# One more slot for weight slabs, taken from two chunk tiles, and a later rounding of the first unit's second slab

## The chip, the cores and the metric

The kernel runs on one core of a Trainium2 chip. The metric is the device time of one execution, in microseconds (us). Five engines work side by side, each through its own instructions in order: TensorE (PE, matmuls; PEld is its weight loads), VectorE (DVE), ScalarE (ACT), GpSimd (POOL) and SyncE (SP). Engines wait for each other by semaphores. SP and POOL issue most of the DMA transfers here.

## What is computed

The reference is one decoder layer on a sequence of 512 rows of width 1024, in fp32:

```python
# h = x + 1/2 * SwiGLU_1(rmsnorm(x))                # D_FF = 2816
# u = rmsnorm(h);  z = u @ W_in -> conv GLU | q | k | v | merge gates
# branch A: GLU -> causal depthwise conv (31 taps) -> LayerNorm -> swish -> C->D
# branch B: dilated causal window attention, 12 heads in 3 groups -> D
# h = h + W_o( sigmoid(gA) * yA + sigmoid(gB) * yB )
# h = h + 1/2 * SwiGLU_2(rmsnorm(h))
# h = h + sigmoid(rmsnorm(h) @ W_pg) * (p @ W_pp)
# y = rmsnorm_final(h)
def swiglu(x, w_gate, w_up, w_down):
    return (jax.nn.silu(x @ w_gate) * (x @ w_up)) @ w_down
```

The change alters no arithmetic.

## The kernel before, in words

**Precision.** PE multiplies rounded fp32 ("fp32r"). Each operand is split in a rounded high part and a remainder, and each product is made of three: high by high, high by low, low by high. `wr` is a raw weight slab, `wh` and `wl` its high and low part; `xsh` and `xsl` are those of an activation chunk `u`. The simple way to split is ACT's copy to `wh` (L398, L419, L540) and DVE's subtraction to `wl` (L399, L420, L541).

**The FFNs.** Each runs after the same list, PLAN: rounds `gate_up(j)` ("gu", j = 2 to 10), rounds `down` ("dn") and two rounds `down_plain` ("dp"); the two gate_up rounds ahead of them are made chunk by chunk while the input arrives. The end of the list is `dn 4, dp 0, gu 10, dp 1, dn 5`. A gate_up round multiplies with a scheme of seven products in place of eight, in the order B11, B21, T2, T1, T3, B22, T4 (`quarters_of`, L745, L746 for the high parts of the weights and L748 for the low ones; results in the PSUM banks pa, pe and pd). Behind each product ACT copies the bank (L943), or DVE adds the bank to an earlier copy (L956); L961, L965 and L966 scale, apply silu and multiply; L948 takes T4. What comes out is cut again into the forms that `down` needs by L676, L688 and L691. `down` runs the same seven products (L755, L756, L760) and DVE adds to the residual (L769, L771). `down_plain` is plain (PE L1004, L1005, L1008; DVE L1013).

**Weights.** `load_one` sends the quarters of a weight to raw slabs from SP's queue (L267). `sum_one` makes the sums that the seven products need on DVE (L336, L340, L344, L349). Products T2, T1, T3, B22 are split by L398 and L399. For B11, B21, T4 and dp the low part is made by DMA: ACT writes the negated high part to `wl` (L368), POOL issues a transfer that adds the raw slab to it (L370, the accumulating DMA), and ACT writes `wh` (L382).

**Slots.** All of these slabs, and the products `u`, come from one ring in on-chip memory: tag "w", `NW` slots of 128 x 1024 fp32, 4 KB a partition. Activation chunks come from a second ring, tag "t", `NT` slots of 128 x 512, 2 KB a partition. A tile that is asked for takes the free slot that was released first, and its first writer waits for whoever used the slot last. So an instruction can wait for an engine or a DMA whose data it never touches.

**Order.** The order of the instructions of each engine is that of the program as it is written (the scheduler is manual). Work beside the products is put between them by budgets (`work`, `spend`) that do not depend on the number of slots.

**The start.** `begin` loads eight input chunks and the first unit's two slabs on SP's and ACT's queues, and for each chunk `scaled` makes `u` (ACT L497) and `xsh`, `xsl` (DVE L498, L499). The slabs are rounded in three parts between them (`part`, L540 on ACT, L541 on DVE): part 0 is chunks 0 and 1 of the first slab, part 1 chunks 2 and 3, part 2 the whole second slab, which serves chunks 4 to 7.

Of the kernel before, what the change touches and what calls it, by code (L numbers as in the profile page):

```python
# [39 lines left out]
MAGIC = float(0x5F3759DF)  # L40


NT = 61
SLAB = 1024
NW = 16
RAW = 4
AHEAD = 2

# [101 lines left out]
def block_kernel(ctx: ExitStack, tc: tile.TileContext, a, out):  # L150
# [12 lines left out]
    def name(n):  # L163
        count[0] += 1
        return f"{n}_{count[0]}"

    def T(n, dt=F32, w=S):
        return act.tile([P, w], dt, name=name(n), tag="t", bufs=NT)

    def by_class(t):

        return t.rearrange("p (i c) -> p c i", c=NB)
# [24 lines left out]
    def quarter(n, step, q):  # L199

        x_, y = divmod(q, 2)
        if step[0] == "gu":
            w = a["w_ffn%s_%s" % (n, ("gate", "up")[x_])]
            return row_of([w[c][:, y * S:(y + 1) * S] for c in chunks(step[1])])
        if step[0] == "mx":
            return rows("w_mix_out", x_, 4 * y + 2 * step[1])
        return rows("w_ffn%s_down" % n, x_, 2 * ROUNDS[step[1]][0] + 2 * y)
# [50 lines left out]
    def W(n, dt=F32):  # L258
        return wts.tile([P, SLAB], dt, name=name(n), tag="w", bufs=NW)

# [18 lines left out]
    def load_one(hold=False):  # L279
        i = state["load"]  # L280
        key = order[i]
        q = product(key)
        if key[0] == "gq" or q is None:
            raws[i] = fetch(sources(key), first_=key[0] in POOLED or key[0] == "gq" and by_dma(key), hold=hold)
        elif q == "B11":
            for z in (A21, A22, A11):
                quarters[key[:2], z] = fetch(quarter(key[0], key[1], z))
        elif q == (MIXED if key[0] == "m" else PRODUCTS)[1]:
            quarters[key[:2], A12] = fetch(quarter(key[0], key[1], A12))
        state["load"] = i + 1  # L290
# [97 lines left out]
    def split_one():  # L388
        i = state["split"]
        if i in halves:  # L390
            state["split"] = i + 1
            return
        r, q, kind = raws.pop(i), product(order[i]), order[i][0]
        if q is not None:
            w = r.shape[-1]
            h, l = W("wh", F32R)[:, :w], W("wl", F32R)[:, :w]
            spend(0.25 + w * 0.00075, 0.17 + w * 0.001)
            A.activation(h, r, AF.Copy)  # L398
            V.tensor_sub(l, r, h.bitcast(F32))  # L399
            halves[i] = h, l  # L400
        elif kind == "pg":
            hs, ls, low = [], [], W("wl", F32R)
            for c in range(2):
                z = r.rearrange("p (m k i) -> p k m i", k=2, i=P)[:, c]
                h, l = T("pgh", F32R), low[:, c * S:(c + 1) * S]
                hm, lm = (t.rearrange("p (m i) -> p m i", i=P) for t in (h, l))
                A.activation(hm, z, AF.Copy)
                V.tensor_sub(lm, z, hm.bitcast(F32))
                hs.append(h)
                ls.append(l)  # L410
            halves[i] = (hs, ls)
        else:
            w = r.shape[-1]
            h, l = W("wh", F32R)[:, :w], W("wl", F32R)[:, :w]
            halves[i] = (h, l)
            if kind == "pT":
                r = r.rearrange("p (k i c) -> p k c i", k=2, c=NB)
                h, l = (z.rearrange("p (k c i) -> p k c i", k=2, c=NB) for z in (h, l))
            A.activation(h, r, AF.Copy)  # L419
            V.tensor_sub(l, r, h.bitcast(F32))  # L420
        state["split"] = i + 1
# [72 lines left out]
    def scaled(src, n, scale, by=lambda t: t):  # L494

        u, h, l = T("u"), T(n + "h", F32R), T(n + "l", F32R)
        A.activation(by(u), src, AF.Copy, scale=scale)  # L497
        V.tensor_copy(h, u)  # L498
        V.tensor_sub(l, u, h.bitcast(F32))  # L499
        return u, (h, l)  # L500
# [19 lines left out]
    def gain(v, c):  # L520
        return gains[:, v + c:v + c + 1]

    def begin():

        rs_ = [W("wr") for _ in range(2)]
        hl = [(W("wh", F32R), W("wl", F32R)) for _ in rs_]
        x = [res[:, :S] if c == 0 else T("x") for c in range(KD)]
        xs, us = [], {}
        cuts = [[(0, slice(0, 256)), (0, slice(512, 768))], [(0, slice(256, 512)), (0, slice(768, 1024))],
                [(1, slice(0, 512)), (1, slice(512, 1024))]]  # L530

        def piece(j, queue):
            for i, c in cuts[j]:
                g, at = divmod(c.start, S)
                src = quarter("1", ("gu", 0), (A11, A12)[i])[g][2]
                queue.dma_start(rs_[i][:, c], src[:, at:at + c.stop - c.start])

        def part(j):
            for i, c in cuts[j]:
                A.activation(hl[i][0][:, c], rs_[i][:, c], AF.Copy)  # L540
                V.tensor_sub(hl[i][1][:, c], rs_[i][:, c], hl[i][0][:, c].bitcast(F32))  # L541

        nc.sync.dma_start(gx[:, :V_DW + S], a["gx"])
        piece(0, nc.scalar)
        for c in range(1, KD):
            nc.sync.dma_start(x[c], a["xT"][c - 1])
            if c in (1, 3):
                piece((c + 1) // 2, nc.sync)
        nc.sync.dma_start(ident, a["eye"])
        state["load"] = state["sum"] = state["early"] = state["split"] = 2  # L550
        load_one()
        load_one()
        nc.sync.dma_start(taps, a["taps"])
        nc.sync.dma_start(freq, a["cst"][:, C_M[NG]:C_M[NG] + 1])
        for c in range(KD):
            us[c], z = scaled(by_class(x[c]), "xs", gain(V_G1, c), classes)
            xs.append(z)
            if c < 3:
                part(c)
            if c == HOLD:  # L560
                load_one(True)
            if c == KD - 1:
                split_one()
        halves[0], halves[1] = hl
        return x, xs, us
# [487 lines left out]
    def tables():  # L1053
        ip = act.tile([P, S], I32, name="ipos", tag="t", bufs=NT)
        nc.sync.dma_start(ip, bass.AP(tensor=a["positions"].tensor, offset=a["positions"].offset, ap=[[0, P], [1, S]]))
        ang, n, nh, nl, e = T("ang"), T("n"), T("nh", F32R), T("nl"), T("e")
        sin, cos = e, nl
        tabs["sin"], tabs["cos"] = sin, cos
        c = TWO_PI

        def do(f, *p, **q):
            bg.append(lambda: f(*p, **q))

        def less(t, k, w):
            do(V.scalar_tensor_tensor, t, k, -w, t, op0=OP.mult, op1=OP.add)

        def reduce(t):
            do(V.tensor_scalar, n, t, 1.0 / (2.0 * math.pi), ROUND, op0=OP.mult, op1=OP.add)
            do(V.tensor_scalar, n, n, -ROUND, None, op0=OP.add)
            for w in c[:3]:  # L1070
                less(t, n, w)

        do(V.tensor_copy, classes(ang), by_class(ip))
        do(V.tensor_scalar, ang, ang, freq, None, op0=OP.mult)
        do(V.tensor_scalar, ip, ang, 1.0 / (2.0 * math.pi), None, op0=OP.mult)
        do(V.tensor_copy, n, ip)
        do(V.tensor_copy, nh, n)
        do(V.tensor_sub, nl, n, nh.bitcast(F32))
        hi = nh.bitcast(F32)
        for k, w in ((hi, c[0]), (nl, c[0]), (hi, c[1])):  # L1080
            less(ang, k, w)
        do(V.tensor_scalar, e, nl, -c[1], None, op0=OP.mult)
        less(e, hi, c[2])
        reduce(ang)
        reduce(e)
        do(V.tensor_add, ang, ang, e)
        for k, w in ((nl, c[2]), (hi, c[3]), (nl, c[3])):
            less(ang, k, w)
        reduce(ang)
        do(V.tensor_scalar, ang, ang, 3.1415925, -3.1415925, op0=OP.min, op1=OP.max)  # L1090

        def end():
            A.activation(sin, ang, AF.Sin)
            V.scalar_tensor_tensor(n, ang, -1.0, ang, op0=OP.mult, op1=OP.max)
            V.tensor_scalar(n, n, -1.0, math.pi / 2, op0=OP.mult, op1=OP.add)
            A.activation(cos, n, AF.Sin)
            V.tensor_scalar(sin[0:64], sin[0:64], -1.0, None, op0=OP.mult)
        bg.append(end)


    norm = Rows()
    x, xs, u1 = begin()

    def row_block(b, j):
# [475 lines left out]
    for j in range(4):  # L1580
        wh, wl = slab(("ao", j))
        for i in range(2):
            m = 2 * j + i
            p = bank("pb")
            for kk in range(4):
                c = slice((4 * i + kk) * P, (4 * i + kk + 1) * P)
# [220 lines left out]
```

## Time and profile before

| what | us |
|---|---|
| median of 3 runs | 1279.35 |
| lowest and highest | 1276.61, 1281.44 |
| profiled execution | 1279.57 |
| its span | 1277.8 |
| PE busy in it | 1261.8 |

The span runs from the first to the last instruction that the profile has; 1.8 us of the execution lie around it. All times in the trace count from the span's start. FFN1 takes about the first 350 us, the mixing stage runs to about 840, FFN2 to about 1200, and the embedding and the last norm to the end. In rows of the timeline the columns are start, length, engine, line, operation, output and inputs by tile names without numbers, how many were grouped, and in brackets the idle time before it and what ended it.

### The profile page before, as it was taken

The numbers are of one execution on the slowest core, as the hardware profiler recorded it, in microseconds if no ns is written. First come the engines' busy times: TensorE is split into PE (matmuls) and PEld (weight loads), VectorE is DVE, ScalarE is ACT, GpSimd is POOL, SyncE is SP. The second block draws the span as 40 slices with busy tenths as digits, with TensorE's granted clock in tenths as the row PEclk, the third lists the DMA queues.
The fourth block names the chain that finished last, engine by engine and source line by source line (L and its number), as shares of the span: only waits on it lengthen the run. The fifth ranks groups of instructions, "written<-read, shape, count | busy, mean of one in ns | idle before, by whom it ended". The sixth has DMA issues, their size and how long they took to land.

```text
span 1277.8 us, 19737 instructions
## 1 busy us (share of the span) xinstructions
PE 1261.8 (99%) x7394; PEld 1118.8 (88%) x7394; DVE 1051.6 (82%) x1713; ACT 743.3 (58%) x1084; POOL 237.7 (19%) x310
## 2 busy tenths in 40 slices
PE   9999999999999999999999999999999999999997
PEld 7898999998888889889898888878898999998886
DVE  6898988897889988888888654797688988897975
ACT  6576666575643354747565545465576666665563
POOL 0011111111222232323332222124111111111000
PEclk9999999999999999999999999999999999999999
DMA  7378778688788899888888777759677778677531
GB/s 270 83 169 211 167 184 202 157 195 217 171 188 203 187 181 193 158 187 153 173 176 190 170 165 184 196 128 278 140 163 199 173 186 207 156 201 184 149 99 66
DMA packets 121702, 225.45 MB, mean 176 GB/s; under 512 B 19208, under 2 KB 63624, under 8 KB 121608
## 3 DMA queue, kind: packets, MB, share of 16 engines
q0 software_dynamic: 48160, 141.58, 54.3%
q1 hardware_dynamic: 73160, 82.37, 20.2%
q8 instruction: 58, 0.95, 0.3%
q14 instruction: 36, 0.29, 0.1%
q10 hardware_dynamic: 288, 0.26, 0.1%
HBM read 168.56 MB, written 2.13 MB: 134 GB/s over the span
## 4 chain that ended last, share of the span: by engine, by line
PE 88%; DVE 5%; DMA 2%; issue 2%; ACT 2%; DVEq 0%; POOLq 0%; ACTq 0%
PE pa L748 5%; PE pa L745 5%; PE pa L746 5%; PE pq L470 4%; PE pq L471 4%; PE pq L472 4%; PE pg L471 3%; PE pg L470 3%; PE pg L472 3%; PE pa L755 3%; PE pa L756 3%; PE pa L760 3%; PE pd L746 2%; PE pd L748 2%; PE pd L745 2%
## 5 line engine op out<-in xcount | busy, mean ns | idle before, releaser
L370 POOL DMA_DIRECT2D wl<-wr x98 | 84.6, 863 | 606.1 <-ACT wl L368 433.2
L1154 DVE SCALAR_TENSOR_TENSOR acc<-glu,taps,acc 128x511 f32<-128x511 f32 (+14 forms) x240 | 161.3, 733 | 0.0
L399 DVE TENSOR_TENSOR wl<-s,wh 128x1024 fp32r<-128x1024 f32 x90 | 109.9, 1221 | 41.6 <-ACT wh L398 32.2
L368 ACT ACTIVATE wl<-wh 128x1024 fp32r<-128x1024 f32 x84 | 87.9, 1051 | 72.8 <-DMA wh<-in_w_in 41.3
L368 ACT ACTIVATE wl<-wr 128x1024 fp32r<-128x1024 f32 x98 | 102.9, 1050 | 17.6 <-DVE wl L399 6.8
L745 PE MATMUL pa<-bh,wh 128*128 128x256 f32 x432 | 106.8, 285 | 3.2 <-DVE p L956 3.2
L382 ACT ACTIVATE wh<-wr 128x1024 fp32r<-128x1024 f32 x98 | 102.6, 1047 | 10.4 <-PE pd L760 7.4
L746 PE MATMUL pa<-bl,wh 128*128 128x256 f32 x432 | 106.7, 284 | 0.0
L398 ACT ACTIVATE wh<-s 128x1024 fp32r<-128x1024 f32 x90 | 94.0, 1049 | 21.2 <-PE pd L756 9.5
L370 POOL DMA_DIRECT2D wl<-in_w_in x56 | 48.7, 870 | 225.4 <-ACT wl L368 219.9
L470 PE MATMUL pq<-xsh,wh 128*128 128x512 f32 x224 | 88.7, 396 | 0.0
L471 PE MATMUL pq<-xsl,wh 128*128 128x512 f32 x224 | 87.3, 390 | 0.0
L472 PE MATMUL pq<-xsh,wl 128*128 128x512 f32 x224 | 87.3, 390 | 0.0
L745 PEld LDWEIGHTS pa<-bh,wh 128*128 128x128 f32 x432 | 83.3, 193 | 3.6 <-DVE p L956 3.6
L746 PEld LDWEIGHTS pa<-bl,wh 128*128 128x128 f32 x432 | 83.5, 193 | 0.0
L470 PE MATMUL pg<-xsh,wh 128*128 128x512 f32 x192 | 76.9, 401 | 0.3 <-DVE tg L831 0.2
L471 PE MATMUL pg<-xsl,wh 128*128 128x512 f32 x192 | 75.3, 392 | 0.7 <-DVE xsl L499 0.6
L472 PE MATMUL pg<-xsh,wl 128*128 128x512 f32 x192 | 75.0, 391 | 0.0
L943 ACT ACTIVATE p<-pa 128x512 f32<-128x512 f32 x36 | 21.5, 596 | 74.4 <-PE pa L748 74.0
L748 PE MATMUL pa<-bh,wl 128*128 128x256 f32 x432 | 61.4, 286 | 0.0
L771 DVE SCALAR_TENSOR_TENSOR gx<-pa,half,gx 128x512 f32<-128x512 f32 x80 | 56.3, 747 | 1.6 <-PE pa L760 1.3
L748 PEld LDWEIGHTS pa<-bh,wl 128*128 128x128 f32 x432 | 56.5, 195 | 0.0
(363 smaller groups left out, 3829.7 us busy)
## 6 DMA issues: line engine op xcount, KB each, us to landing
wl<-wr POOLq DMA_DIRECT2D x98, 512.0 KB, 5.2
wh<-in_w_in POOLq DMA_DIRECT2D x56, 512.0 KB, 7.3
wl<-in_w_in POOLq DMA_DIRECT2D x56, 512.0 KB, 6.5
wr<-in_w_ffn_down SPq DMA_DIRECT2D x44, 512.0 KB, 5.3
wr<-in_w_ffn_up SPq DMA_DIRECT2D x80, 256.0 KB, 4.5
wr<-in_w_ffn_gate SPq DMA_DIRECT2D x78, 256.0 KB, 4.9
wh<-in_w_v POOLq DMA_DIRECT2D x16, 256.0 KB, 7.1
wl<-in_w_v POOLq DMA_DIRECT2D x16, 256.0 KB, 5.1
```

What stands on the lines that cost most here:

```text
L368: A.activation(l.bitcast(F32R), h, AF.Copy, scale=-1.0)
L370: G.dma_start(to, src, accum_op=OP.add)
L382: A.activation(h, r, AF.Copy)
L398: A.activation(h, r, AF.Copy)
L399: V.tensor_sub(l, r, h.bitcast(F32))
L470: PE.matmul(ps, wh, xh, start=start, stop=False, skip_group_check=part)
L471: PE.matmul(ps, wh, xl, start=False, stop=False, skip_group_check=part)
L472: PE.matmul(ps, wl, xh, start=False, stop=stop, skip_group_check=part)
L745: PE.matmul(o, h[:, c], th, start=q in ("B11", "B21", "T1") and i == 0, stop=False, skip_group_check=True)
L746: PE.matmul(o, h[:, c], tl, start=False, stop=False, skip_group_check=True)
L748: PE.matmul(o, l[:, c], th, start=False, stop=i >= len(at) - 2, skip_group_check=True)
L1154: bg.append(lambda acc=acc, g=g, w=w, s=s: V.scalar_tensor_tensor(acc[:, s:], g[:, :S - s], w, acc[:, s:], op0=OP.mult, op1=OP.add))
```

## The change

`NW` goes from 16 to 17 and `NT` from 61 to 59 (17 x 4 + 59 x 2 KB is what 16 x 4 + 61 x 2 was). In `begin`, part 2 is written behind the fourth chunk in place of behind the third.

```diff
-NT = 61
+NT = 59
 SLAB = 1024
-NW = 16
+NW = 17
...
             us[c], z = scaled(by_class(x[c]), "xs", gain(V_G1, c), classes)
             xs.append(z)
-            if c < 3:
-                part(c)
+            if c in (0, 1, 3):
+                part((c + 1) // 2)
```

The number of instructions of every engine stays as it was. At the start DVE's order is another one (before, then now; `wl_103` is the second slab's low part, `u_160` or `u_164` the fourth chunk, `u_170` the fifth):

```order
L541 TENSOR_TENSOR wl_103<-wr_99,wh_102 128x512 x2
L498 CAST xsh_165<-u_164 128x512
L499 TENSOR_TENSOR xsl_166<-u_164,xsh_165 128x512
L498 CAST xsh_171<-u_170 128x512
L499 TENSOR_TENSOR xsl_172<-u_170,xsh_171 128x512
```

```order
L498 CAST xsh_161<-u_160 128x512
L499 TENSOR_TENSOR xsl_162<-u_160,xsh_161 128x512
L541 TENSOR_TENSOR wl_103<-wr_99,wh_102 128x512 x2
L498 CAST xsh_171<-u_170 128x512
L499 TENSOR_TENSOR xsl_172<-u_170,xsh_171 128x512
```

The fourth chunk's two instructions moved ahead of the second slab's two; on ACT its L497 moved ahead of L540 in the same way.

Everywhere else the order stays and the slots change, and with them the waits. In each FFN's round gu 10, ACT before and now (the waits are semaphores: DMAHW of loads from SP's queue, DMASW of POOL's transfers; `wr_3353` is the dp slab's raw one, `pd_3479` the bank of B22):

```order
L398 ACTIVATE wh_3470<-s_546_3314 128x1024
L368 ACTIVATE wl_3474<-wr_3353 128x1024 [waits DMAHW6_49,DVE_49]
L382 ACTIVATE wh_3475<-wr_3353 128x1024 [waits PE_49]
L943 ACTIVATE p_3504<-pd_3479 128x512 [waits PE_49]
L688 ACTIVATE bh_3537<-t_3506 128x512 [waits DVE_49]
```

```order
L398 ACTIVATE wh_3470<-s_546_3314 128x1024 [waits Activation_49]
L368 ACTIVATE wl_3474<-wr_3353 128x1024 [waits DMAHW6_49,DMASW7_49,Activation_49]
L382 ACTIVATE wh_3475<-wr_3353 128x1024 [waits DVE_49]
L943 ACTIVATE p_3504<-pd_3479 128x512 [waits PE_49]
L688 ACTIVATE bh_3537<-t_3506 128x512 [waits DVE_49]
```

and DVE there, before and now:

```order
L399 TENSOR_TENSOR wl_3471<-s_546_3314,wh_3470 128x1024 [waits DMASW7_49,DMASW2_49,Activation_49]
L676 TENSOR_TENSOR t_3506<-u_2901 128x256
L676 TENSOR_TENSOR t_3506<-u_2901,t_3387 128x256
L691 TENSOR_TENSOR bl_3428<-t_3387,bh_3427 128x512
L336 TENSOR_TENSOR s_582_3510<-wr_3434,wr_3436 128x1024 [waits DMAHW7_49,DMAHW0_49,PE_49]
L956 TENSOR_TENSOR p_3504<-p_3504,pa_3355 128x512 [waits PE_49,Activation_49]
```

```order
L399 TENSOR_TENSOR wl_3471<-s_546_3314,wh_3470 128x1024 [waits PE_49,Activation_49]
L676 TENSOR_TENSOR t_3506<-u_2901 128x256
L676 TENSOR_TENSOR t_3506<-u_2901,t_3387 128x256
L691 TENSOR_TENSOR bl_3428<-t_3387,bh_3427 128x512
L336 TENSOR_TENSOR s_582_3510<-wr_3434,wr_3436 128x1024 [waits DMASW5_49,DMAHW0_49,DMASW2_49,DMAHW7_49,DMASW0_49,PE_49]
L956 TENSOR_TENSOR p_3504<-p_3504,pa_3355 128x512 [waits PE_49,Activation_49]
```

The wait for POOL's transfer on DMASW7 left DVE's L399 and is now on ACT's L368.

On SP's queue, at 250 us, the loads for the next round (before, then now; `wr_2906` is the one issued at 255.01 before):

```order
L267 DMA wr_2693<-in_w_ffn_gate 128x512 [waits DMAHW0_49]
L267 DMA wr_2906<-in_w_ffn_down 128x4x256 [waits DMAHW1_49,PE_49,Activation_49]
L267 DMA wr_2908<-in_w_ffn_down 128x4x256 [waits DMAHW2_49,DMAHW5_49,DMASW6_49,DMAHW6_49,DVE_49,Activation_49]
L267 DMA wr_2910<-in_w_ffn_down 128x4x256 [waits DMAHW3_49,DMASW5_49,PE_49]
L267 DMA wr_2955<-in_w_ffn_down 128x4x256 [waits DMASW7_49,DMAHW4_49,DMASW4_49,PE_49]
```

```order
L267 DMA wr_2693<-in_w_ffn_gate 128x512 [waits DMAHW0_49]
L267 DMA wr_2906<-in_w_ffn_down 128x4x256 [waits DMASW6_49,DMAHW1_49,DVE_49,Activation_49]
L267 DMA wr_2908<-in_w_ffn_down 128x4x256 [waits DMAHW2_49,DMASW7_49,PE_49]
L267 DMA wr_2910<-in_w_ffn_down 128x4x256 [waits DMAHW3_49,DMAHW5_49,DMASW6_49,DMAHW6_49,DVE_49,Activation_49]
L267 DMA wr_2955<-in_w_ffn_down 128x4x256 [waits DMAHW4_49,PE_49,Activation_49]
```

The first of them now waits for DVE where it waited for PE, and the waits of each load have moved on to the next.

## The prediction

> **What bounds the kernel now.** I read the page's first lines, then the busy time by stretches of 40 us, then what TensorE waited for. The page:
>
> ```profile
> span 1277.8 us, 19737 instructions
> PE 1261.8 (99%) x7394; PEld 1118.8 (88%) x7394; DVE 1051.6 (82%) x1713; ACT 743.3 (58%) x1084; POOL 237.7 (19%) x310
> ```
>
> TensorE (PE) is busy for 1261.8 of 1277.8 us, so the change can only win what PE loses. Where that is, the stretches show (columns: length, busy us of PE, PEld, DVE, ACT and POOL, granted clock, DMA share, GB/s):
>
> ```profile
> 0.00:40.00 40.00, 38.08 (x173) 30.52 (x173) 27.07 (x66) 23.96 (x39) 0.20 (x4) 1.00 0.62 216
> 280.00:320.00 40.00, 38.60 (x241) 34.88 (x240) 31.42 (x42) 22.38 (x27) 5.95 (x7) 1.00 0.83 210
> 320.00:360.00 40.00, 39.19 (x198) 32.73 (x198) 34.16 (x61) 26.28 (x43) 9.56 (x14) 1.00 0.71 160
> 1160.00:1200.00 40.00, 37.26 (x236) 34.21 (x236) 30.50 (x44) 23.25 (x32) 4.29 (x5) 0.96 0.59 146
> 1240.00:1280.00 40.00, 29.40 (x153) 25.15 (x151) 22.92 (x66) 12.03 (x28) 0.00 (x0) 0.90 0.14 53
> ```
>
> The last row is the end of the program, which the change does not reach. Of the other 16.0 − 8.4 = 7.6 us that PE is not busy (2.2 us of the last row's 10.6 lie behind the span's end), these four stretches hold 1.92 + 1.40 + 0.81 + 2.74 = 6.87. What ends those waits:
>
> ```profile
> PE pa L745 <- DVE p L956: 3.2, 2, 1.8
> PE pd L748 <- DVE wl L399: 1.0, 1, 1.0
> PE pa L755 <- DVE gx L771: 0.8, 1, 0.8
> ```
>
> The first two are one place, met once in each FFN: the last gate_up round, between the two `down_plain` rounds. PE there, FFN1's rows first, and the stretch of FFN2's slow clock:
>
> ```profile
> 319.24 0.39 PE L745 MATMUL pa<-bh,wh 128*128 128x256 f32 x1 [1.40 <-DVE p L956]
> 322.22 0.40 PE L1004 MATMUL pd<-wh,hidh 128*128 128x512 f32 x1
> ...
> 1178.60 1.21 PE L748 MATMUL pd<-xsh,wl 128*128 128x256 f32 x8 [0.95 <-DVE wl L399]
> 1181.60 0.39 PE L745 MATMUL pa<-bh,wh 128*128 128x256 f32 x1 [1.79 <-DVE p L956]
> 1186.03 0.43 PE L1004 MATMUL pd<-wh,hidh 128*128 128x512 f32 x1
> ```
>
> ```profile
> 1182.70:1186.00 3.30, 3.30 (x17) 3.30 (x17) 3.27 (x5) 1.36 (x2) 0.00 (x0) 0.50 0.74 139
> ```
>
> The T4 product takes 322.22 − 319.24 = 2.98 us in FFN1 and 1186.03 − 1181.60 = 4.43 in FFN2, where the granted clock of the stretch is 0.50: set off by 0.95 + 1.79 us of idle time, it cost 1.45 us. With 1.40 idle in FFN1 the clock held.
>
> Why PE waits: the vector engine (DVE) stands still before L399, and the chain of waits names a transfer:
>
> ```profile
> 307.10 7.74 DMA wl<-wr
> ...
> 1167.85 9.34 DMA wl<-wr
> ```
>
> ```profile
> 314.96 1.23 DVE L399 TENSOR_TENSOR wl<-s,wh 128x1024 fp32r<-128x1024 f32 x1 [3.88 <-DMA wl<-wr]
> 318.51 0.68 DVE L956 TENSOR_TENSOR p<-p,pa 128x512 f32<-128x512 f32 x1
> 1177.32 1.23 DVE L399 TENSOR_TENSOR wl<-s,wh 128x1024 fp32r<-128x1024 f32 x1 [5.48 <-DMA wl<-wr]
> ```
>
> L399 does not read what that transfer writes. It waits because its `wl` was given the slot of a raw slab that POOL's accumulating DMA still reads. Landing is at 314.84 and 1177.19; T4 starts 4.40 us later in both FFNs.
>
> **The change, part by part.** No instruction is added or taken away; nothing needs a price but order and slots. With one slot more, each weight tile takes the slot that the tile before it in the list took until now.
>
> 1. *The last gate_up round.* L399's `wl` now takes a slot that PE released long before (its wait is on PE in the rows shown above), so L399 runs behind its input, at about 311, and the 0.95 us stall of FFN2 goes. But the next tile of the list, ACT's L368 copy, now gets the raw slab's slot, with its wait for the same DMA. Before, these instructions of ACT ran early:
>
> ```profile
> 311.21 1.04 ACT L368 ACTIVATE wl<-wr 128x1024 fp32r<-128x1024 f32 x1
> ...
> 313.10 0.59 ACT L943 ACTIVATE p<-pd 128x512 f32<-128x512 f32 x1
> ```
>
> Queued behind L368 are L382 and L943, and L943's result is what DVE's L956 needs, for which PE's T4 waits. With the same landing: +0.03, then 1.89 (313.10 − 311.21, with L382 between), 0.59 for L943, then L956 to T4 as now, 319.24 − 318.51 = 0.73: T4 starts 3.3 us behind the landing instead of 4.4 (3.24 and a little for the hand over). **That is −1.1 us in each FFN.** DVE meanwhile has its L399, two L676, L691 and L336 done, which before stood between the landing and L956.
>
>    The landing itself may move. Four loads on SP's queue stand around that DMA, and they too get slots about 1 to 2 us earlier. A single accumulating DMA takes 4.5 us with nothing beside it and 6.3 with loads issued 0.5 us behind it, against 7.74 and 9.34 here:
>
> ```profile
> DMA to landing us min/median/max: 4.5/4.5/4.5
> DMA to landing us min/median/max: 6.3/6.3/6.3
> ```
>
> (the first row is L370 issued at 130.4, the second L370 at 161.5). Loads that are over sooner leave a landing earlier by up to 1.4 and 3.0; loads that share longer could leave it where it is. I take little of it: in FFN1 −1.3 in all (the bounds are −1.1 and the whole stall, −1.4), in FFN2 −1.9 (bounds −1.1 and 0.95 + 1.79 = −2.74).
>
>    The half clock of FFN2 then probably does not come, since the idle time left is 0.8 us, less than the 1.40 that did no harm in FFN1. That saves 1.45, but DVE's chain from L956 to the first L771 does not get shorter: FFN1, whose T4 runs at full clock, pays 0.8 there (the L755 row of the waits) and FFN2 pays nothing. So 0.65 at best; I take −0.3. FFN1's 0.8 stays. Late next is the DMA of the waiting L368 tile: so far issued 1.34 us behind L368, then at 316.2, landing 4.5 to 5.5 us later at 320.7 to 321.7; its reader, L1008, runs at 324.06 and then at 322.8, which holds by 1 us:
>
> ```profile
> 312.55 0.85 POOL L370 DMA_DIRECT2D wl<-wr  x1 [4.60 <-ACT wl L368]
> 324.06 1.07 PE L1008 MATMUL pd<-wl,hidh 128*128 128x512 f32 x4
> ```
>
> 2. *Loads come earlier, and share with the DMAs.* In the gate_up round at 250 to 262 two accumulating DMAs follow each other, at 251.50 and 253.40, and SP's load stands 1.6 us behind the second:
>
> ```profile
> 253.40 0.85 POOL L370 DMA_DIRECT2D wl<-wr  x1 [1.05 <-ACT wl L368]
> 255.01 20.54 SPq L267 DMA_DIRECT2D wr<-in_w_ffn_down  x5
> 252.52 0.42 DVE L676 TENSOR_TENSOR t<-u,t 128x256 f32<-128x256 f32 x1
> 260.55 1.12 PE L748 MATMUL pe<-xsh,wl 128*128 128x256 f32 x8
> 1121.21 1.22 PE L748 MATMUL pe<-xsh,wl 128*128 128x256 f32 x8
> ```
>
> ```profile
> DMA to landing us min/median/max: 4.6/5.6/6.7
> DMA to landing us min/median/max: 5.2/6.2/7.2
> DMA to landing us min/median/max: 4.6/5.1/5.7
> ```
>
> These last rows are the pair in FFN1, the same pair in FFN2 (1112.03 and 1113.92), and a pair with no load behind it (292.7 and 294.6).
>
> The load waited for PE's last use of a tile and went out as that ended; its new slot is free at DVE's L676, 252.94, so it goes out 2.0 us earlier. The second DMA took 6.7 and landed at 260.1, and PE's L748 wants it at 260.55: 0.4 to spare. FFN2 has the same pair, with nothing to spare (7.2, and L748 at 1121.21 already 0.2 late). Without a load the second took 5.7. What the load does to the rate:
>
> ```profile
> GB/s 0 0 0 0 0 0 0 0 0 137 191 191 191 164 218 218 218 218 68 150 218 218 205 212 154 89 133 109 109 65 85 178 362 379 386 379 386 382 389 358
> ```
>
> The row is the DMA rate in 40 slices from 250 to 262: about 210 with the DMA alone, 65 to 154 (mean 106) once the load has joined at 257, 360 to 390 for loads alone. What 2.0 us of sharing more costs, no row shows; the bounds: nothing (the load crawls, and the DMA keeps its pace), and twice the time for those 2.0 us, +2.1, so landings of 8.8 and 9.3 and new stalls of 1.7 (FFN1, behind its 0.4) and 2.1 (FFN2). Nearest is a single DMA whose loads come 0.5 us behind it: 6.3 − 4.5 = 1.8 longer. For the second of the pair that is 5.7 + 1.8 = 7.5. I take that: **+0.4 in each FFN**, and no half clock for idle times that short.
>
>    [...]
>
> 3. *The start.* DVE's L541 stood ahead of the fourth chunk's L498 and L499, and PE waited for both:
>
> ```profile
> 9.83 1.28 DVE L541 TENSOR_TENSOR wl<-wr,wh 128x512 fp32r<-128x512 f32 x2
> 12.23 0.50 PE L471 MATMUL pg<-xsl,wh 128*128 128x512 f32 x1 [0.22 <-DVE xsl L499]
> 12.55 0.69 DVE L499 TENSOR_TENSOR xsl<-u,xsh 128x512 fp32r<-128x512 f32 x1
> 13.72 0.39 PE L471 MATMUL pg<-xsl,wh 128*128 128x512 f32 x1
> ```
>
> Now ACT's L497 of the fourth chunk takes the place of L540 and DVE goes on at 9.9 with L498 and L499 (0.42 and 0.69): the chunk is whole at 11.0 and PE runs through it. But L541's 1.28 then stands ahead of the fifth chunk, whose L499 ends at 11.0 + 1.28 + 0.42 + 0.69 = 13.4 where it ended at 13.24, and PE's L471 at 13.72 moves only to 13.4: −0.2 (from 0 to the 0.7 that PE lost in the fourth chunk: it ran its L471 at 12.23, which could start at 11.5).
>
> 4. *Two activation slots fewer.* Only three small loads at 311 to 313, for the mixing stage, get slots 0.2 to 0.5 us later; PE needs them tens of us later. Nothing.
>
> **Sum:** −1.3 − 1.9 − 0.3 + 0.4 + 0.4 − 0.2 = −2.9 us. The profiled execution took 1279.57 (span 1277.8 and 1.8 around it), 0.2 above the median of 1279.35; −2.9 from the median is 1276.5. **I forecast 1276.5 us**, which is no change that a measurement of this kernel tells from none: the three runs span 0.4%, and 0.5% is 6.4 us, so the line is at 1273.0 below and 1285.7 above.
>
> **Rivals.** *The stall changes its engine and nothing is won.* For: the same landing ends a wait in both orders, and two loads now share longer with it, so that landing may come 1.1 later and eat the 1.1. Then 1279.35 − 0.2 + 0.8 = 1280. Against: the loads ahead of the DMA at 307.10 are then over sooner.
>
> *Slower: the earlier loads starve the accumulating DMAs.* Place: L748 of the pair at 253.40 and 1113.92. Price: the upper bounds, 1.7 + 2.1 us of idle time, and behind each a half-clock T product at 1.45, since 2.74 us of idle set it off and 1.40 did not: 6.7, with part 1's gain of 2.2 gone if the landings there come 1.1 later too. 1279.35 + 6.7 − 0.2 = 1286. It decides from a landing of about 8.5 us on. For: the rate row, 106 against 210. Against: loads already stand 0.5 us behind single DMAs (161.5) and cost 1.8, not 2.1 on top.
>
>    [...]
>
> *Faster by over 0.5%.* All waits at the last round go (−1.4 − 2.74 − 0.65), the start wins its 0.7, no DMA lengthens, and FFN1's 0.8 at L771 goes as the chain ahead of it is earlier, with half of the 0.75 us that PE loses elsewhere: −6.7, 1272.7. Against: DVE is busy without a break from 318.51 to that L771, so its 0.8 does not depend on the stall.
>
> **How the numbers follow.** Forecast 0.60 (its own range 1274 to 1279), no gain 0.24, slower 0.08, faster 0.08. The bounds of the terms give 1279.35 − 5.5 = 1273.9 and 1279.35 − 2.2 + 3.8 + 2.9 = 1283.9; the range is 1273 to 1284. Faster by over 0.5% 0.08, within 0.84, slower 0.08.
>
> **What would show it.** In the changed kernel's trace: ACT's L368 at about 314.9 with an idle time before it ended by the DMA, and DVE's L399 at about 311; T4 at 317.9 to 318.2 where it stood at 319.24; full clock through FFN2's T4; SP's L267 at 253.0 where it stood at 255.01; and the second DMA of the pair at 7 to 8 us with 0.4 us before L748. The forecast is wrong if that DMA takes over 8.5 us, if a half clock stands where none stood, or if L368's wait comes out as long on PE as L399's.

## The result, and the profile after

The change is slower: 1288.26 us (median of 4 runs, 1287.36 to 1289.08) against 1278.83 before, measured beside it (4 runs), a ratio of 1.0073 with an interval of 1.0052 to 1.0094. The forecast was 1276.5, and the range ended at 1284.0. The profiled execution took 1288.9.

The page of the changed kernel, and its busy time by stretches (columns as before the change: length, busy us of PE, PEld, DVE, ACT and POOL, granted clock, DMA share, GB/s):

```profile
span 1287.0 us, 19687 instructions
PE 1264.0 (98%) x7394; PEld 1120.9 (87%) x7394; DVE 1051.7 (82%) x1713; ACT 742.8 (58%) x1084; POOL 237.8 (18%) x310
```

```profile
240.00:280.00 40.00, 39.36 (x315) 38.62 (x315) 34.94 (x48) 29.77 (x40) 5.10 (x6) 1.00 0.67 160
280.00:320.00 40.00, 35.90 (x215) 31.99 (x214) 30.83 (x40) 20.84 (x25) 5.10 (x6) 0.98 0.79 198
320.00:360.00 40.00, 39.78 (x205) 34.70 (x206) 31.68 (x46) 24.54 (x40) 8.53 (x12) 0.94 0.76 171
1120.00:1160.00 40.00, 37.90 (x252) 34.92 (x252) 33.93 (x45) 25.47 (x31) 4.58 (x6) 1.00 0.80 196
1160.00:1200.00 40.00, 35.58 (x227) 33.08 (x226) 29.02 (x41) 19.99 (x27) 4.85 (x6) 0.91 0.69 162
```

PE lost 1.40 us at 280 to 320 and now loses 4.10; it lost nothing at 1120 to 1160 and now loses 2.10. The prediction had named both places. At the first, the last gate_up round, it forecast a gain and a loss came; at the second, product B21, it forecast a small loss and a larger one came. What ended PE's waits:

```profile
PE pd L745 <- ACT p L943: 8.7, 2, 4.4
PE pe L748 <- DMA wl<-wr: 2.7, 2, 2.1
```

The first row is new. Before, PE waited at T4 for DVE's L956 (3.2 us) and at B22 for L399 (1.0); both are gone, and PE now waits 8.7 us at the *first* matmul of B22, for ACT's copy L943. ACT in that round (timeline):

```profile
311.20 1.05 ACT L398 ACTIVATE wh<-s 128x1024 fp32r<-128x1024 f32 x1
317.68 1.06 ACT L368 ACTIVATE wl<-wr 128x1024 fp32r<-128x1024 f32 x1 [5.44 <-issue]
318.65 1.04 ACT L382 ACTIVATE wh<-wr 128x1024 fp32r<-128x1024 f32 x1
319.59 0.58 ACT L943 ACTIVATE p<-pd 128x512 f32<-128x512 f32 x1
```

L368 stood 5.44 us, as the prediction had it, with L382 and L943 behind it; the row names no releaser, but the DMA issued at 308.03 landed 9.6 us later (below), at 317.6. But the copy p<-pd is that of product T1, and the next product in that bank is B22, which adds to what stands there. So B22, and not T4 one product later, has to wait for it: 319.59 + 0.58 = 320.17, and PE starts at 320.22. PE before (first fence) and after:

```profile
314.81 0.28 PE L745 MATMUL pd<-xsh,wh 128*128 128x256 f32 x1
334.10 0.47 PE L755 MATMUL pa<-wh,bh 128*128 128x512 f32 x1 [0.81 <-DVE gx L771]
1175.56 0.28 PE L745 MATMUL pd<-xsh,wh 128*128 128x256 f32 x1
```

```profile
261.39 0.39 PE L748 MATMUL pe<-xsh,wl 128*128 128x256 f32 x1 [0.64 <-DMA wl<-wr]
320.22 0.58 PE L745 MATMUL pd<-xsh,wh 128*128 128x256 f32 x1 [4.32 <-ACT p L943]
325.30 0.28 PE L745 MATMUL pa<-bh,wh 128*128 128x256 f32 x1
339.08 0.39 PE L755 MATMUL pa<-wh,bh 128*128 128x512 f32 x1
1128.44 0.50 PE L748 MATMUL pe<-xsh,wl 128*128 128x256 f32 x2 [2.10 <-DMA wl<-wr]
1187.37 0.58 PE L745 MATMUL pd<-xsh,wh 128*128 128x256 f32 x1 [4.42 <-ACT p L943]
1195.26 0.40 PE L1004 MATMUL pd<-wh,hidh 128*128 128x512 f32 x1
```

By the same instruction in both traces, the changed kernel stands behind the old one by this much:

| PE instruction | before | after | behind by |
|---|---|---|---|
| B21's L748, FFN1 | 260.55 | 261.39 | 0.84 |
| B22's first L745, FFN1 | 314.81 | 320.22 | 5.41 |
| T4's first L745, FFN1 | 319.24 | 325.30 | 6.06 |
| L755 behind L771, FFN1 | 334.10 | 339.08 | 4.98 |
| B21's L748, FFN2 | 1121.21 | 1128.44 | 7.23 |
| B22's first L745, FFN2 | 1175.56 | 1187.37 | 11.81 |
| first L1004 behind T4, FFN2 | 1186.03 | 1195.26 | 9.23 |
| the span | 1277.8 | 1287.0 | 9.2 |

So +0.8 at B21 and +4.1 net in the last gate_up round of FFN1, +2.3 up to B21 of FFN2 (the wait there is 2.1 of it) and +2.0 net in FFN2's last round: 9.2 in all. Inside the last gate_up round the new wait alone put PE some 4.5 us further behind in each FFN. In FFN1 the half clock behind it put 2.2 more on top (at B22's last matmul the changed kernel stood 7.6 behind), and the old waits at T4 and L771 gave 1.6 and 1.1 back. The half clock lasted 6.8 us, now in both FFNs, where FFN2's lasted 3.4 before (1182.68 to 1186.10; stretches, with a clock of 0.50):

```profile
318.20:325.00 6.80, 4.78 (x22) 4.78 (x23) 2.42 (x3) 4.38 (x6) 1.70 (x2) 0.50 0.68 130
1185.20:1192.00 6.80, 4.63 (x21) 4.63 (x22) 2.43 (x3) 4.53 (x6) 1.71 (x2) 0.50 0.66 125
```

The accumulating DMAs got longer. In order: the pair at 251.55 and 253.45, the one at 308.03, the pair at 1117 and 1119, the one at 1175.09.

```profile
DMA to landing us min/median/max: 5.5/6.7/7.9
DMA to landing us min/median/max: 9.6/9.6/9.6
DMA to landing us min/median/max: 5.8/7.6/9.4
DMA to landing us min/median/max: 9.7/9.7/9.7
```

Before they took 4.6 and 6.7, 7.7, 5.2 and 7.2, and 9.3.

How that comes about, the two kinds of traffic show (q0 is POOL's accumulating DMA, q1 SP's loads; packets, MB, share of the engines in the stretch). In the changed kernel from 256 to 257.5, then from 257.5 to 260.5, and from 309.2 to 311.8:

```profile
q1 hardware_dynamic: 373, 0.38, 72.9%
q0 software_dynamic: 16, 0.00, 0.9%
...
q0 software_dynamic: 123, 0.50, 86.7%
q1 hardware_dynamic: 236, 0.23, 23.7%
...
q1 hardware_dynamic: 862, 0.85, 100.9%
```

From 256 to 257.5 the load that went out at 253.06 moved 0.38 of its 0.52 MB, while the second DMA, issued at 253.45, moved no data (the 16 packets of q0 there hold 0.00 MB). And from 309.2 to 311.8 the loads alone moved 0.85 MB, while the DMA issued at 308.03 moved nothing. Three loads had gone out ahead of it, at 304.42, 306.38 and 307.30, and the third landed at 312.4; in the kernel before only two had, at 305.44 and 306.36 against 307.10.

In these rows the accumulating DMA moved nothing while loads that had gone out ahead of it moved 0.38 and 0.85 MB. By an estimate from 0.52 MB and the 360 to 390 GB/s that loads alone had (the rate row in the prediction), each such load costs it about 1.4 us. From 313.5 to 315.5 both moved: the DMA 90 packets with 0.36 MB, the loads 89 with 0.09.

### The profile page after: what moved, and what is told of

The parts are those of the page before. It is cut to its first block, busy times and chain, and to the rows that moved or that the text cites. A ratio compares the mean times of both kernels' runs of the same rounds, so it can differ in the third digit from the quotient of the medians.

```text
span 1287.0 us, 19687 instructions
## 1 busy us (share of the span) xinstructions
PE 1264.0 (98%) x7394; PEld 1120.9 (87%) x7394; DVE 1051.7 (82%) x1713; ACT 742.8 (58%) x1084; POOL 237.8 (18%) x310
## 5 line engine op out<-in xcount | busy, mean ns | idle before, releaser
L399 DVE TENSOR_TENSOR wl<-s,wh 128x1024 fp32r<-128x1024 f32 x90 | 109.9, 1221 | 36.4 <-ACT wh L398 36.4
L368 ACT ACTIVATE wl<-wh 128x1024 fp32r<-128x1024 f32 x84 | 87.9, 1051 | 66.4 <-DMA wh<-in_w_in 37.5
L368 ACT ACTIVATE wl<-wr 128x1024 fp32r<-128x1024 f32 x98 | 103.0, 1051 | 34.3 <-DMA wr<-in_w_ffn_gate 11.1
L746 PE MATMUL pa<-bl,wh 128*128 128x256 f32 x432 | 106.0, 283 | 0.0
L745 PE MATMUL pa<-bh,wh 128*128 128x256 f32 x432 | 106.0, 283 | 0.0
L382 ACT ACTIVATE wh<-wr 128x1024 fp32r<-128x1024 f32 x98 | 102.5, 1046 | 1.1 <-PE pd L756 0.8
L471 PE MATMUL pq<-xsl,wh 128*128 128x512 f32 x224 | 87.3, 390 | 0.0
L746 PEld LDWEIGHTS pa<-bl,wh 128*128 128x128 f32 x432 | 82.9, 192 | 0.0
L745 PEld LDWEIGHTS pa<-bh,wh 128*128 128x128 f32 x432 | 82.9, 192 | 0.0
L471 PE MATMUL pg<-xsl,wh 128*128 128x512 f32 x192 | 75.2, 392 | 0.7 <-DVE xsl L499 0.4
L943 ACT ACTIVATE p<-pa 128x512 f32<-128x512 f32 x36 | 21.5, 596 | 82.3 <-PE pa L748 81.9
L748 PE MATMUL pa<-bh,wl 128*128 128x256 f32 x432 | 60.6, 283 | 0.0
L771 DVE SCALAR_TENSOR_TENSOR gx<-pa,half,gx 128x512 f32<-128x512 f32 x80 | 56.3, 748 | 2.6 <-PE pa L760 2.3
L748 PEld LDWEIGHTS pa<-bh,wl 128*128 128x128 f32 x432 | 55.7, 192 | 0.0
```

What stands on the lines that cost most here:

```text
L368: A.activation(l.bitcast(F32R), h, AF.Copy, scale=-1.0)
L471: PE.matmul(ps, wh, xl, start=False, stop=False, skip_group_check=part)
L745: PE.matmul(o, h[:, c], th, start=q in ("B11", "B21", "T1") and i == 0, stop=False, skip_group_check=True)
L746: PE.matmul(o, h[:, c], tl, start=False, stop=False, skip_group_check=True)
L748: PE.matmul(o, l[:, c], th, start=False, stop=i >= len(at) - 2, skip_group_check=True)
```

## The experiments

Ten runs. "Before" in each group is the kernel before, run on the same chip beside them: 1279.41 for the first four, 1278.55 for the next four, 1278.90 for the last two.

### The two parts of the change apart

```diff
# e1: the slots alone
-NT = 61
+NT = 59
-NW = 16
+NW = 17
# e2: the moved rounding alone
-            if c < 3:
-                part(c)
+            if c in (0, 1, 3):
+                part((c + 1) // 2)
```

> The 17th slot and the two chunk tiles fewer, with the second slab's rounding where it was. Theory A (all of the loss comes from the slots): the same stalls as in the change, about 4.5 us ahead of B22 in the last gate_up round of each FFN, each with a half clock behind it, and 0.8 and 2.2 us at B21's L748; time 1288.2 to 1288.6. Rival (the moved rounding has a share): under 1286.

> The moved rounding alone, with 16 and 61 slots. Theory A: the fifth chunk's matmuls 0.1 to 0.3 us earlier and nothing else, 1278.5 to 1278.9 beside 1278.8 before. Rival: a loss of 1 us or more.

Measured: the slots alone 1289.26 us, ratio 1.0081 (1.0066 to 1.0096), with the same waits (8.2 us at B22, 2.6 at B21). The moved rounding alone 1278.53, ratio 0.9997 (0.9986 to 1.0008). So the whole loss is that of the slots, and what the rounding is worth is too little for the times to show. The traces show it: in the changed kernel PE stood 0.27 us behind the old one in the third chunk (L471 at 10.23 against 9.96), because a load landed later in that execution (L540 at 5.71 against 5.45), and 0.04 in the sixth (15.13 against 15.09), which is a gain of 0.23. In the run with the moved rounding alone the same two lags are 0.77 and 0.50, a gain of 0.27.

### T1's copy out from behind the wait

The change, with the second `down_plain` slab's L368 and L382 written one product later, behind T1's L943:

```diff
-if j - i > (LEAD.get(product(order[j]), 9) if product(order[j]) else 5 if order[j][0] == "dp" else lead):
+if j - i > (LEAD.get(product(order[j]), 9) if product(order[j]) else (3 if order[j][3] else 5) if order[j][0] == "dp" else lead):
```

> The change, with the second down_plain slab's L368 and L382 written one product later, so that they stand behind T1's copy L943 on ACT; L368 still waits for the same DMA. Theory B (the 4.5 us are the copy p<-pd that stands in the queue behind the waiting L368, and that B22 needs because it overwrites the bank pd): no wait of PE ahead of B22, no half clock, the wait of L368 as long as before, and only a smaller wait (2 to 3 us in FFN1) at L755 further on, as L688 still stands behind it; B21's waits stay; 1280 to 1282. Rival (PE would wait as long anyway, because DVE or the DMA is late for T4): a wait of 3 us or more ahead of T4 in place of that ahead of B22, 1286 or more.

Measured: 1283.19, ratio 1.0023 (1.0011 to 1.0036). ACT in that round:

```profile
312.97 0.60 ACT L943 ACTIVATE p<-pd 128x512 f32<-128x512 f32 x1 [0.81 <-PE pd L748]
317.00 1.06 ACT L368 ACTIVATE wl<-wr 128x1024 fp32r<-128x1024 f32 x1 [3.43 <-DMA wl<-wr]
318.91 0.61 ACT L688 ACTIVATE bh<-t 128x512 fp32r<-128x512 f32 x1
```

PE's waits now read

```profile
PE pa L755 <- DVE gx L771: 3.7, 2, 2.1
PE pe L748 <- DMA wl<-wr: 2.6, 2, 1.9
```

The wait at B22 is gone, the one at T4 with it, though L368 waits for the same late DMA until 317.00. That settles the mechanism: what cost 4.3 and 4.4 us was the copy's place in ACT's queue. What was late next is L688, also behind L368, and through DVE's chain L771, 3.7 us where 2 to 3 in one FFN were expected. In FFN2 the wait of 1.93 us at B21 had slow matmuls behind it, which was not expected: L745 and L746 stood 0.21 us apart from 1125.25 to 1128.24, as at the clock of 0.50 in the changed kernel, and not 0.12 as before the wait. The 16 of them from 1124.96 on took 3.28 us where 16 at 0.12 take 1.92; by this estimate 1.4 us, which covers the 1.2 by which the time came out above what was expected.

### Two slots more

```diff
-NT = 61
-NW = 16
+NT = 57
+NW = 18
```

with the moved rounding.

> 18 and 57 slots, with the moved rounding. By the rule that each tile takes the slot its predecessor had, the late raw slab's slot goes one tile further, to ACT's L382, with L368 free to run early. Theory B: B22 waits one ACT copy less, 0.95 to 1.0 us in each FFN, that is about 3.5 us in place of 4.5, with the half clock still there; 1286 to 1286.8. Rival (the wait is set by something else than the place in ACT's queue): 4.5 us again, 1288. B21's DMA at 253.4: two loads at its start where one was, landing 7.9 us or later.

Measured: 1278.59, ratio 0.9998 (0.9987 to 1.0009), 8 us less than expected. The slot went where the rule sends it: L368 is free, and now L382 waits.

```profile
315.56 1.06 ACT L382 ACTIVATE wh<-wr 128x1024 fp32r<-128x1024 f32 x1 [2.06 <-DMA wl<-wr]
316.52 0.58 ACT L943 ACTIVATE p<-pd 128x512 f32<-128x512 f32 x1
```

But the DMA itself took 7.1 us in FFN1 and 6.2 in FFN2, not 9.6 and 9.7:

```profile
DMA to landing us min/median/max: 7.1/7.1/7.1
DMA to landing us min/median/max: 6.2/6.2/6.2
```

From 309.2 to 311.8 it moved 0.09 MB and the loads 0.55, where in the changed kernel it moved nothing and the loads 0.85. B22 waits 1.0 us, in FFN1 only, and no half clock follows it (behind 317.15 the matmuls stand 0.12 us apart). That the wait would move on by one copy was expected; that the DMA's own length would go with the slots was not.

### Holding loads back

To move the loads away from a DMA and change nothing else, three of them, the first three quarters of one down round, get a one-column memset on DVE in their raw slab first, so that SP has to wait for DVE's place in the program (`fetch` has this memset, L265, for the start):

```diff
-quarters[key[:2], z] = fetch(quarter(key[0], key[1], z))
+quarters[key[:2], z] = fetch(quarter(key[0], key[1], z), hold=key[1] == ("dn", 4))
```

e5 holds round 4's loads, e6 those of round 5, e7 both; all with 17 slots.

> The change, with three of SP's loads (the first three quarters of the fourth down round) held back by a one-column memset of each raw slab on DVE, so that in both FFNs they go out about 6 us later, behind the two accumulating DMAs of B11 and B21 in the round ahead. Nothing else moves. Theory C (the loads beside it lengthen B21's DMA): it takes 5.4 to 5.9 us as a pair with no load does, L748 of B21 waits for nothing in FFN1 and FFN2, the round gu 10 is as bad as in the change; 1285 to 1286 beside 1288.3 to 1289.3. Rival (the second DMA of a pair is long for another reason): 7.9 and 9.2 us as in the change, 1288 to 1289.

> The change, with the same hold on the first three quarters of the fifth down round instead, which go out about 3.4 us behind the accumulating DMA of the first down_plain slab where they stood around it. Theory C: this DMA takes 5 to 6 us where it took 9.6, so ACT's L368 waits until about 313.5 and not 317.6; B22 waits 0.5 to 1.5 us where it waited 4.5, no half clock in either FFN; 1278.5 to 1281. If the loads now come too late for DVE's L336, 1 to 2 us more, ahead of T4. Rival (the wait is long for the DMA's own length): 4 us and the half clocks stay, 1287 to 1289.

> Both holds. Theory C: the two effects add, 1275 to 1278, faster than the kernel before by 0.1 to 0.3%, with no wait of PE over 1.5 us between 20 and 1190 us. Rival: the one hold's loads run into the other DMA, 1279 or more.

Measured, the pair at 251 in e5 and the DMA at 307.6 in e6:

```profile
DMA to landing us min/median/max: 4.6/5.0/5.4
```

```profile
DMA to landing us min/median/max: 4.5/4.5/4.5
```

5.4 where it was 7.9, and 4.5 where it was 9.6: the loads were the whole of what lengthened these DMAs. In e6 no wait at B22 was left. But the times were 1289.14 (ratio 1.0072, 1.0054 to 1.0089), 1282.23 (1.0026, 1.0014 to 1.0038) and 1282.12 (1.0030, 1.0016 to 1.0043), all above what was expected. In e5 and e7 the held loads ran into the next DMA of that kind, at 262.6 and 262.9, which took 9.0 and 8.9 us where it had taken 6.0. In e5 DVE's L340 waited 1.0 us for it, so the DMA that POOL issues behind L340 went out late, and PE waited for that one:

```profile
279.85 1.21 PE L760 MATMUL pa<-wl,b 128*128 128x512 f32 x4 [1.35 <-DMA wl<-wr]
```

In e6 they came too late for DVE's sums:

```profile
316.70 1.23 DVE L336 TENSOR_TENSOR s<-wr,wr 128x1024 f32<-128x1024 f32 x1 [2.32 <-DMA wr<-in_w_ffn_down]
```

with 1.7 us at T4 and 2.3 at L771. So theory C holds for the DMAs and fails for the time (e5's is the rival's, though for another reason): here a load held back was late for its reader or in the next DMA's way.

### Eighteen slots with holds, and with T1's copy freed

> 18 and 57 slots with the hold on the fourth down round's quarters. With 18 slots alone B21's L748 waited 1.2 and 1.7 us with a half clock behind the second. Theory C: both waits and that half clock go, 1278.6 - 1.2 - 1.7 - 1.7 = 1274, the least of all runs. Rival: 1277 or more, because held loads are late for the fourth down round's sums.

> 18 slots with the hold on the fourth down round's quarters, and the second down_plain slab's L368 and L382 written behind T1's copy. Theory B: the two waits of B22 for L943 that are left, 2.3 us in all, go; DVE's chain up to L771 is only some 0.5 us earlier, so 0.5 to 0.9 us of each comes back at L755; 1273 to 1274.5 beside 1275.0 without it. Rival: all of it comes back, 1275 or more.

e8 is 18 and 57 slots with the hold on round 4's loads; e9 has e3's edit as well. Measured: e8 1274.97, ratio 0.9961 (0.9946 to 0.9976); e9 1273.00, ratio 0.9953 (0.9938 to 0.9968). e9 came in its range, and e8 1 us above the 1274 that was expected and below its rival's 1277. e9 beats both kernels, by 0.5% against the one before. The intervals of e8 and e9 overlap, so the times alone do not show what e3's edit adds; the traces do: e8 has 2.3 us of waits at B22 and e9 none. The 1.6 us that PE waited for a DMA at L760 in e5 are gone in e8, with the same hold and 18 slots. What is left in e9:

```profile
PE pa L755 <- DVE gx L771: 0.9, 1, 0.9
PE pa L745 <- DVE p L956: 0.6, 1, 0.6
```

```profile
280.00:320.00 40.00, 40.00 (x253) 36.38 (x252) 34.74 (x46) 23.56 (x28) 5.95 (x7) 1.00 0.86 211
320.00:360.00 40.00, 40.00 (x199) 33.63 (x198) 34.14 (x67) 26.29 (x43) 11.84 (x16) 1.00 0.76 170
1120.00:1160.00 40.00, 40.00 (x240) 35.77 (x239) 37.01 (x48) 23.77 (x27) 6.00 (x7) 1.00 0.93 224
1160.00:1200.00 40.00, 39.14 (x247) 35.08 (x246) 34.23 (x49) 26.67 (x36) 4.29 (x5) 1.00 0.74 188
```

PE loses 0.86 us in these four stretches together; the kernel before lost 4.95 there, the changed one 10.84 (its 0.22 at 320 to 360 with a clock of 0.94).

### The hold without the slots

The kernel before with the hold on round 5's loads alone.

> The kernel before (16 and 61 slots, rounding where it was) with only the hold on the fifth down round's quarters. Theory C: the accumulating DMA ahead of the last gate_up round takes 4.5 us in place of 7.7 and 9.3, DVE's L399 no longer waits for it, and most of the waits at B22 and T4 and the half clock of FFN2 go; the held loads make L336 and L771 later, as in the run with 17 slots, where that round gained 0.2 us on the kernel before in FFN1 and about 2.2 in FFN2; 1276 to 1277.5. Rival: the waits stay as long, 1278.5 or more.

Measured: 1285.01, ratio 1.0047 (1.0029 to 1.0066), slower where faster was expected. The DMA took 4.5 us and L399 ran at 311.82, as expected. But DVE then stood for the held loads twice:

```profile
316.54 1.23 DVE L336 TENSOR_TENSOR s<-wr,wr 128x1024 f32<-128x1024 f32 x1 [2.22 <-DMA wr<-in_w_ffn_down]
321.71 1.23 DVE L340 TENSOR_TENSOR s<-s,wr 128x1024 f32<-128x1024 f32 x1 [2.75 <-DMA wr<-in_w_ffn_down]
```

and the four loads, now close together, went out ahead of the next accumulating DMA, which took 8.8 us from 312.67. The mean granted clock of that execution was 0.995 (0.998 in e9's). PE waited 2.5 us at L771 in FFN1, and in FFN2 at T4:

```profile
PE pa L745 <- DVE p L956: 5.1, 2, 4.6
```

So with 16 slots the hold took the loads from one DMA and put them ahead of another.

## Why the prediction was wrong

**The step that failed** is the first one, "L943's result is what DVE's L956 needs, for which PE's T4 waits", with its sum, "T4 starts 3.3 us behind the landing instead of 4.4". That the wait would move from DVE's L399 to ACT's L368 with L382 and L943 behind it was right, to the instruction. Its sum from the landing to L943's end was right too, 0.03 + 1.89 + 0.59 = 2.5 us: 317.6 to 320.17. But L943 copies T1's result out of a bank that B22 writes next, so the first who waits for it is PE's B22, one product ahead of T4. With the landing of before, 314.84, B22 would have started at 317.35 and not at 314.81: 2.5 us lost, of which T4's 1.4 come back. What was put down as a gain of 1.1 us at T4 was a loss of 1.1 before anything else. In FFN2 the same sum gives 1177.19 + 2.5 = 1179.7 against 1175.56: 4.1 of the 4.4 us that B22 now waits there come from this step alone. The text ahead of the prediction calls that bank the bank of B22: true, but the copy in the row reads it *before* B22 does. The mistake could have been seen in the trace of before: L943 at 313.10 stands ahead of PE's B22 at 314.81 in pd, and in the kernel T2 and T3 add to the bank pa behind a copy in the same way.

**The landing** was the second error of that step. "Loads that are over sooner leave a landing earlier by up to 1.4 and 3.0" took the earlier loads as a help; the DMA took 1.9 us more in FFN1 (9.6 against 7.7) and 0.3 more in FFN2. The first load came 2 us earlier against the DMA (3.6 us ahead of it where it had been 1.7), but the loads were not over when it went out: three stood ahead of it in place of two, and from 309.2 to 311.8 it moved no data. e6 and e10 show 4.5 us where nothing is ahead of it. In FFN2 there were three in place of two as well; that it had taken 9.3 us there already, with two, no run here explains.

**Together** in FFN1: a landing 1.9 later, the copy's reader one product sooner, and a half clock. Of FFN2's the prediction said that it "probably does not come"; with idle times of 4.3 and 4.4 us one came in both FFNs. The prediction also put FFN2's half clock of before down to 0.95 and 1.79 us of idle time together; the 0.95 ended at 1178.60 and the clock fell at 1182.68, and no run shows what each of the two did to it. The three signs of being wrong that the prediction named all came: the second DMA over 8.5 us (in FFN2), a half clock where none stood (in FFN1), and L368's wait on PE.

**B21's DMAs** ("+0.4 in each FFN") had the right mechanism and the wrong size: PE waited 0.6 us there in FFN1 and 2.1 in FFN2. The price was taken from a DMA whose loads come 0.5 us *behind* it; with a load 0.4 us ahead of it (253.06 against 253.45) it took 7.9 us, not 7.5, and in FFN2 9.4, just over the upper bound of 9.3. The upper bound, twice the time for as long as both move, was the better number for FFN2, but the rows show no one rate of sharing: from 313.5 to 315.5 the DMA moved 90 packets beside the loads' 89, and in the 2.6 us from 309.2 the loads moved 862 and the DMA none.

**The start** (−0.2) was right, 0.23 by the traces, and for **the chunk slots** (nothing) no wait of PE shows.

**The rivals.** The slower rival named the starved DMAs and 1286, which is nearest to the time, with 8 in 100. It had the B21 part right in FFN2 (2.1 against 2.1) and too long in FFN1 (1.7 against 0.6), the half clocks that it put behind them did not come, and it did not have the part that cost most. So it is by luck that its sum is near. PE's waits of 4.3 and 4.4 us had a half clock, and the 2.10 us at 1128 had none, but in e3 the wait of 1.93 us at the same place had one (last table). The length of a wait alone does not tell them apart.

## What to carry to other kernels

In a ring of slots that are handed out in the order of release, one slot more moves a wait for a slot to the next tile (here from L399 to L368, and with 18 slots to L382); so the question is not how many slots there are, but which instruction inherits the latest release, and what stands behind it in its engine's queue. For each such instruction, look for the first reader *or overwriter* of what is queued behind it, the banks of PE included. And more room makes loads earlier, which is a gain only if they do not then stand ahead of a transfer that somebody waits for.

## What the runs showed of the hardware

- An accumulating DMA of 512 KB took 4.5 us alone, 5.4 to 5.7 as the second of a pair, and in the rows above 6.2 to 9.7 with loads ahead of it or beside it; in one stretch of 2.6 us (309.2 to 311.8 in the changed kernel) these moved 862 packets and it moved none. A hold of the loads brought 7.9 to 5.4 (e5) and 9.6 to 4.5 (e6).
- Loads that came in while such a DMA ran moved little beside it: in the changed kernel from 313.5 to 315.5 the DMA 90 packets and 0.36 MB, the loads 89 and 0.09. In the kernel before, from 257 to 259:

```profile
q0 software_dynamic: 57, 0.23, 108.1%
q1 hardware_dynamic: 18, 0.02, 3.4%
```

- The granted clock fell to 0.50 at some of PE's waits and not at others (the clock of e3 and e4 is read from how far apart the matmuls of L745 and L746 stand, 0.21 us at 0.50 and 0.12 at 1.00 in the changed kernel):

| run, place | PE went on at | wait, us | granted clock |
|---|---|---|---|
| before, T4 in FFN1 | 319.24 | 1.40 | 1.00 |
| before, B22 and T4 in FFN2 | 1178.60 and 1181.60 | 0.95 and 1.79 | 0.50 from 1182.68 to 1186.10 |
| changed, B22 in FFN1 | 320.22 | 4.32 | 0.50 from 318.20 to 325.03 |
| changed, B22 in FFN2 | 1187.37 | 4.42 | 0.50 from 1185.19 to 1192.01 |
| changed, B21 in FFN1 | 261.39 | 0.64 | 1.00 |
| changed, B21 in FFN2 | 1128.44 | 2.10 | 1.00 |
| e3, B21 in FFN2 | 1123.91 | 1.93 | matmuls 0.21 us apart from 1125.25 to 1128.24 |
| e4, B22 in FFN1 | 317.15 | 0.95 | matmuls 0.12 us apart |

By these rows the length of a wait does not tell whether a half clock comes: the 2.10 us had none, and the 1.93 at the same place in e3 had one. What tells the two apart they do not show.
